# Splitting the next layer's q, k and v columns beside the second MLP product and keeping them in device memory

## The chip, the cores and the metric

The kernel runs on one NeuronCore of a Trainium2 chip. Its instructions stand in five queues, each worked off in order: TensorE (PE in the profile) multiplies matrices, VectorE (DVE) and GpSimd (POOL) do elementwise arithmetic, ScalarE (ACT) does copies and activation functions, SyncE (SP) issues every DMA of this kernel. An instruction starts when it is at the head of its queue and the semaphores that it waits for have come. The metric is the device time of one execution in microseconds (us).

## The reference, cut to what matters

Two encoder layers on 1024 positions of width 1024, in float32. A layer is a token mixing that starts with `u = x @ w_in[l]`, an output product with a LayerNorm, and an MLP with a LayerNorm:

```python
for l in range(DEPTH):                              # DEPTH = 2
    u = x @ w_in[l]
    u_f, q_b, k_b, v_b, u_c, q_d, k_d, v_d = jnp.split(u, pts, axis=-1)
    ...                                             # four kinds of mixing -> y
    x = layer_norm(ALPHA * x + y, ln1_g[l], ln1_b[l])
    h = jnp.square(jax.nn.relu(x @ w_ff1[l]))
    x = layer_norm(ALPHA * x + h @ w_ff2[l], ln2_g[l], ln2_b[l])
```

The case turns on the border between the layers: the end of `h @ w_ff2[0]` with its LayerNorm, and the first products of layer 1, `x @ w_in[1][:, 256:512]` (all of `q_b`) and `x @ w_in[1][:, 512:768]` (`k_b` and `v_b`).

## The kernel before, in words

Every float32 operand of a product is split into a high part that TensorE takes (`F32R`) and a low part, the rest; a product is then three matmuls, hi by hi, hi by lo and lo by hi (`mm3`, lines 172 to 176, shown as L174, L175, L176). A split is `split` (L167): a cast on ACT (L168) gives the high part, a subtraction (L169) on VectorE or GpSimd the low part.

The second MLP product (`ff_down`) uses Strassen's seven products. The 4096 rows of `w_ff2` are taken in 4 chunks, each chunk takes 7 steps in the order `DOWN = (1, 2, 6, 5, 3, 7, 4)`, so there are 28 steps, i = 0 to 27. A step is 4 tiles of 12 matmuls of 512 columns, each tile summed in one of 6 PSUM banks (`x`), and VectorE adds each tile to a running sum (L1540) and so frees its bank. A step needs an operand A (1 MB of hidden values, loaded from `h_scratch` and split in `down_a`, L1414 to L1421: cast on ACT, the first two quarters of the subtraction on GpSimd, the other half on VectorE) and an operand W (split by L168 and L169 on ACT and VectorE from blocks of `w_ff2`). There are three places for each: the operands of step i+3 go where those of step i were, so the load of the next A (`w<-h_scratch` or `T<-h_scratch`) is issued when a step ends, and it serves the step three later.

In the last chunk the sums get their last additions with a running total of each row (`total`, L1440), and then each tile of 128 rows is normalized (`norm`, L1443, and `normalize`, L185: a square on ACT with a sum, L189, a square root, L190, and on VectorE L191, L192 and twice L194, each half stored to `x_scratch`). The tiles 0 to 3 are done after the steps 3 and 7 of the last chunk, the tiles 4 to 7 after its last step. In the order in which the program stands on VectorE, the totals and the norms are mixed with each other.

At the start of the last step the columns of `q_b` for the next layer are loaded into four tiles `raw` (256 KB each; the pool has four such buffers) and split into a tile `w` of a pool with two buffers; the two are also the A operands of the last steps. The columns of `k_b` and `v_b` are loaded into the same four `raw` buffers, and are split at the start of the next layer. These splits use ACT (`CAST w<-raw`) and GpSimd (`TENSOR_TENSOR w<-raw,w`). Then the rows are turned by transposes on TensorE (`back`, L224: L220, and a split from PSUM into `T` on ACT and VectorE), and for each tile of rows comes the product with the columns of `q_b`, three tiles later that with the columns of `k_b` and `v_b` (`mix`, from L336). The order inside each queue is set when the program is built, from the program's order and a schedule; it can differ from the order of the lines.

Of the kernel before, what the change touches and what calls it, by code (L numbers as in the profile page):

```python
# [16 lines left out]
F32R = mybir.dt.float32r  # L17
# [5 lines left out]
P = 128  # L23
# [3 lines left out]
KT = D // P  # L27
DEPTH = 2
# [80 lines left out]
class Trunk:  # L109
    def __init__(self, ctx, tc, a):  # L110
        self.tc, self.nc, self.a = tc, tc.nc, a
        nc = self.nc
        perm = ctx.enter_context(tc.tile_pool(name="perm", bufs=1, side="right"))
        self.ws = ctx.enter_context(tc.tile_pool(name="ws", bufs=1, side="right"))
        self.ps = ctx.enter_context(tc.tile_pool(name="ps", bufs=1, space=PSUM))
        self.ahead = None
        self.T = perm.tile([P, KT, 2, S], F32R, name="T")
        self.ident = perm.tile([P, P], F32, name="ident")
        self.eps = perm.tile([P, 2], F32, name="eps")
        nc.vector.memset(self.eps[:, 0:1], LN_EPS)  # L120
        nc.vector.memset(self.eps[:, 1:2], RMS_EPS)

        def scratch(name, *shape):
            return nc.dram_tensor(name, shape, F32, kind="Internal").ap()

        self.xs = scratch("x_scratch", S, D)
        self.bs = scratch("bias_scratch", 4, P * RL)
        self.ms = scratch("merge_scratch", 2, S, 4)

        self.qd = scratch("q_scratch", 8, 2, HD, S)  # L130
        self.kd = scratch("k_scratch", 6, 2, HD, S)
        self.vd = scratch("v_scratch", S, 6, 2, HD)

        self.tabs = scratch("dft_scratch", 4, P, 2, 2, 2, 2 * P)

        self.hs = scratch("h_scratch", 7, PAIRS, P, 512)


# [106 lines left out]
    def split_cols(self, raws):  # L245
# [2 lines left out]
            self.split(W[:, 2 * i:2 * i + 2, 0], W[:, 2 * i:2 * i + 2, 1], raw, self.nc.gpsimd)  # L248
        return W

    def load_cols(self, w, c0):
        return self.split_cols(self.fetch_cols(w, c0))

# [79 lines left out]
        self.dma(self.vd[t * P:(t + 1) * P, h0:h0 + n], v)  # L333


    def mix(self, l, Wq, raws, before):  # L336
        nc, tc, a = self.nc, self.tc, self.a
        w_in = a["w_in"][l]
        g, v = nc.gpsimd, nc.vector
        with ExitStack() as c:  # L340
# [4 lines left out]
            if Wq is None:  # L345
                Wq = self.load_cols(w_in, 256)
# [4 lines left out]
            for t in range(NT + KLAG):  # L351
                if t < NT:
                    step()
                    o = self.tm([Wq], t)
                    nc.scalar.copy(qk[:, t, 0:4].rearrange("p a b -> p (a b)"), o)
                if t == 0:
                    Wk = self.split_cols(raws or self.fetch_cols(w_in, 512))
                if t == NT:
                    gate = self.load_cols(w_in, 1024)
                if t >= KLAG:  # L360
                    o = self.tm([Wk], t - KLAG)
                    nc.scalar.copy(qk[:, t - KLAG, 4:6].rearrange("p a b -> p (a b)"), o[:, 0:128])
                    self.put_values(sm, o[:, 128:256], t - KLAG, 0, 2)
# [1061 lines left out]
    def ff_down(self, l, places, w2, last, p0, b11):  # L1425
# [8 lines left out]
        junk = kp.tile([P, D], mybir.dt.bfloat16, name="junk")  # L1434
        mvs = [kp.tile([P, 4], F32, name=f"mv{t}") for t in range(NT)]
        out = a["out"] if last else self.xs
        Wq, raws = None, None


        def total(t, j, y):  # L1440
# [7 lines left out]
        with ExitStack() as c:  # L1448
# [58 lines left out]
            for i in range(steps):  # L1507
                ch, n = i // 7, DOWN[i % 7]
                final = ch == steps // 7 - 1
                A, W = places[i % 3]  # L1510
                if final and n == 4 and not last:
                    Wq = self.split_cols(self.fetch_cols(a["w_in"][l + 1], 256))
                    raws = self.fetch_cols(a["w_in"][l + 1], 512)
                if final and n == 7:
                    held = []
                for t in range(4):

                    both = final and n == 4
                    o = held[t] if both else acc.tile([P, 512], F32, tag="x", name="x", bufs=6)
                    for j in range(CHUNK):  # L1520
                        self.mm3(o, [A[:, j, k, t * P:(t + 1) * P] for k in (0, 1)], [W[:, j, k] for k in (0, 1)],
                                 j == 0 and not both, j == CHUNK - 1, both or final and n == 7)
                    r = R[n][t]
                    if ch == 0 and n in (2, 3, 7):
                        v.scalar_tensor_tensor(r, residual(t + 4 * (n == 7), int(n != 2)), ALPHA, o, OP.mult, OP.add)
                    elif ch == 0 and n == 4:

                        y, z = residual(t + 4, 0), residual(t + 4, 1)
                        g.tensor_tensor(y, y, z, OP.subtract)
                        v.scalar_tensor_tensor(r, y, ALPHA, o, OP.mult, OP.add)  # L1530
                    elif ch == 0:
                        act.copy(r, o)
                    elif final and n in (3, 7, 4):
                        total(t + 4 * (n != 3), int(n != 4), o)
                        if n == 3:
                            norm(t)
                        if n == 7:
                            held.append(o)
                    else:
                        v.tensor_tensor(r, o, r, OP.add)  # L1540
                    if not final:
                        continue
                    if n == 1:
                        g.tensor_tensor(R[4][t], R[4][t], R[7][t], OP.add)
                    if n == 2:
                        total(t, 0, R[1][t])
                    if n == 6:
                        v.tensor_tensor(r, r, R[1][t], OP.add)  # L1548
                        g.tensor_tensor(R[4][t], R[4][t], r, OP.add)
                    if n == 5:  # L1550
                        v.tensor_tensor(r, r, R[6][t], OP.add)  # L1551
                        v.tensor_tensor(R[3][t], R[3][t], r, OP.add)  # L1552
                        g.tensor_tensor(R[7][t], R[7][t], r, OP.add)
                if 3 <= i + 3 < steps:
                    prepare2(i + 3)
                if final and n == 1:
                    for k, y in enumerate(("ln2_g", "ln2_b")):
                        self.dma(gb[:, k], a[y][l].rearrange("(o d) -> o d", o=1).to_broadcast([P, D]))
# [14 lines left out]
        if last:  # L1573
            for t in range(4, NT):
                norm(t)
            keep.close()
            return None, None, None
        return Wq, raws, tail()


@with_exitstack
def encoder_kernel(ctx, tc, a):
    tr = Trunk(ctx, tc, a)
    Wq, raws, before = None, None, tr.embed()
    for l in range(DEPTH):
        psum = ExitStack()
        psum.enter_context(tr.wide())
        with tr.third():
            Wo = tr.mix(l, Wq, raws, before)
        Wo = tr.attention(l, Wo)  # L1590
        psum.enter_context(tr.third())
        Wq, raws, before = tr.ff(l, Wo, psum, l == DEPTH - 1)


# [25 lines left out]
```

## Time and profile before

| | us |
|---|---|
| median of 3 runs | 2331.02 (2330.0 to 2331.39) |
| the profiled execution | 2328.44 |
| its span, first to last instruction | 2326.3 |
| PE busy | 2217.1 (95%) |
| DVE busy | 1776.1 (76%) |
| ACT busy | 1077.1 (46%) |
| POOL busy | 793.3 (34%) |

The span is the time from the first to the last instruction of the profiled execution; 2.1 us of the execution lie outside it. TensorE is busy nearly all the time, so the time of the kernel is the time of its matmuls and of the waits in between. The second MLP product of layer 0 ends at about 1171 us of the span, in the middle of it. A row of a timeline gives start, duration, engine, line, operation, what is written and read, how many equal instructions were merged, and in brackets how long the engine had been idle and who released it.

### The profile page before, as it was taken

How to read it: one execution, taken by the hardware profiler on the slowest of the kernel's cores; microseconds unless marked ns; L12 is line 12 of the kernel's file. 1: busy time of each engine (PE TensorE's matmuls, PEld its weight loads, DVE VectorE, ACT ScalarE, POOL GpSimd, SP SyncE). 2: the span in 40 equal slices, each digit the busy share in tenths (PEclk: the TensorE clock that was granted, in tenths of full speed). 3: DMA queues.
4: the chain of work that ended last, by engine and by line, in shares of the span. 5: the costliest groups of instructions: out<-in, count | busy, mean ns of one | idle time of the engine just before them, and what ended most of it. 6: DMA issues, size and time to landing. Idle time of an engine off the chain costs nothing. (4 is left out here: it accounts for less than half of the span.)

```text
span 2326.3 us, 31019 instructions
## 1 busy us (share of the span) xinstructions
PE 2217.1 (95%) x11212; PEld 1869.2 (80%) x11212; DVE 1776.1 (76%) x2500; ACT 1077.1 (46%) x1851; POOL 793.3 (34%) x540
## 2 busy tenths in 40 slices
PE   7999899998999999999989999999899999999997
PEld 6888887976778887888788798788677788788886
DVE  7687667968776777778957966788787767776699
ACT  3343767845333344333333446677443333443333
POOL 2361203016332233435514702110262333354353
PEclk9999999999999999999999999999999999999999
DMA  8444673043344467644223539621343444765433
GB/s 312 127 124 149 190 197 117 19 154 116 137 160 162 159 223 261 205 142 134 98 92 98 153 114 260 171 83 58 125 147 132 165 163 158 276 217 175 160 100 109
DMA packets 222950, 357.44 MB, mean 154 GB/s; under 512 B 21416, under 2 KB 100716, under 8 KB 221708
## 3 DMA queue, kind: packets, MB, share of 16 engines
q1 hardware_dynamic: 222796, 355.45, 47.1%
q8 instruction: 89, 1.46, 0.3%
q14 instruction: 65, 0.53, 0.1%
HBM read 244.44 MB, written 115.15 MB: 155 GB/s over the span
## 5 line engine op out<-in xcount | busy, mean ns | idle before, releaser
L174 PE MATMUL x<-T,w 128*128 128x512 f32 x1088 | 425.5, 393 | 12.2 <-DVE x L1441 4.7
L176 PE MATMUL x<-T,w 128*128 128x512 f32 x1088 | 425.0, 391 | 4.0 <-POOL w L169 2.6
L175 PE MATMUL x<-T,w 128*128 128x512 f32 x1088 | 426.2, 392 | 2.8 <-DVE T L169 2.8
L174 PEld LDWEIGHTS x<-T,w 128*128 128x128 f32 x1088 | 205.3, 189 | 60.8 <-issue 9.7
L176 PEld LDWEIGHTS x<-T,w 128*128 128x128 f32 x1088 | 205.6, 189 | 49.4 <-POOL w L169 3.4
L175 PEld LDWEIGHTS x<-T,w 128*128 128x128 f32 x1088 | 205.7, 189 | 46.7 <-DVE T L169 4.2
L1420 POOL TENSOR_TENSOR w<-w 128x512 fp32r<-128x512 f32 x76 | 147.5, 1961 | 225.1 <-ACT w L1418 225.1
L169 POOL TENSOR_TENSOR w<-raw,w 128x512 fp32r<-128x512 f32 x96 | 138.3, 1466 | 236.7 <-ACT w L168 221.4
L169 POOL TENSOR_TENSOR w<-s,w 128x512 fp32r<-128x512 f32 x68 | 104.3, 1544 | 246.2 <-ACT w L168 165.9
L174 PE MATMUL x<-E,w 128*128 128x512 f32 x384 | 150.6, 392 | 5.9 <-ACT h L1269 4.5
L176 PE MATMUL x<-E,w 128*128 128x512 f32 x384 | 150.1, 392 | 2.0 <-POOL w L169 1.8
L175 PE MATMUL x<-E,w 128*128 128x512 f32 x384 | 150.0, 391 | 0.0
L174 PE MATMUL s<-w,T 128*128 128x256 f32 (+1 forms) x432 | 137.0, 318 | 5.8 <-ACT T L168 5.4
L176 PE MATMUL s<-w,T 128*128 128x256 f32 (+1 forms) x432 | 135.0, 313 | 1.6 <-POOL T L169 1.2
L175 PE MATMUL s<-w,T 128*128 128x256 f32 (+1 forms) x432 | 134.8, 313 | 1.3 <-POOL w L169 1.3
L169 POOL TENSOR_TENSOR w<-rw,w 128x512 fp32r<-128x512 f32 x60 | 93.4, 1573 | 122.5 <-ACT w L168 122.5
L1047 DVE TENSOR_TENSOR s<-rw 128x512 f32<-128x512 f32 x62 | 53.4, 861 | 104.0 <-DMA rw<-in_w_ff_dram 103.7
L1418 ACT CAST w<-w 128x2048 fp32r<-128x2048 f32 x38 | 72.7, 1912 | 129.4 <-DMA w<-h_scratch 122.4
L174 PE MATMUL x<-T 128*128 128x512 f32 x320 | 126.1, 394 | 0.0
L175 PE MATMUL x<-T 128*128 128x512 f32 x320 | 125.5, 392 | 0.0
L176 PE MATMUL x<-T 128*128 128x512 f32 x320 | 125.4, 392 | 0.0
L456 DVE SCALAR_TENSOR_TENSOR o<-hp,cvT,o 128x1024 f32<-128x1024 f32 x88 | 113.3, 1287 | 2.4
(378 smaller groups left out, 5796.5 us busy)
## 6 DMA issues: line engine op xcount, KB each, us to landing
h_scratch<-h SPq DMA_DIRECT2D x224, 256.0 KB, 2.5
w<-h_scratch SPq DMA_DIRECT2D x38, 1024.0 KB, 5.4
rw<-in_w_ff_dram SPq DMA_DIRECT2D x64, 512.0 KB, 5.5
b<-in_w_ff_dram SPq DMA_DIRECT2D x24, 1024.0 KB, 5.5
raw<-x_scratch SPq DMA_DIRECT2D x72, 256.0 KB, 4.7
T<-h_scratch SPq DMA_DIRECT2D x18, 1024.0 KB, 5.3
raw<-in_w_in_dram SPq DMA_DIRECT2D x64, 256.0 KB, 3.5
rw<-in_w_ff_dram SPq DMA_DIRECT2D x10, 1024.0 KB, 5.3
```

The lines of the kernel that those rows point to most:

```text
L169: (lo_eng or self.nc.vector).tensor_tensor(lo, src, hi.bitcast(F32), OP.subtract)
L174: mm(out, l[0], r[0], start=first, stop=False, skip_group_check=more)
L175: mm(out, l[0], r[1], start=False, stop=False, skip_group_check=more)
L176: mm(out, l[1], r[0], start=False, stop=last, skip_group_check=more)
L456: v.scalar_tensor_tensor(o, hp[:, m, k:k + S], cvT[:, m, k:k + 1], o, OP.mult, OP.add)
L1047: eng.tensor_tensor(quad(out), x, y, op)
L1418: nc.scalar.copy(A[:, :, 0], f32)
L1420: nc.gpsimd.tensor_tensor(A[:, j, 1], f32[:, j], A[:, j, 0].bitcast(F32), OP.subtract)
```

## The change

A scratch array in device memory (`w_scratch`) is added. In the steps 8 to 15 of the second MLP product of layer 0, `put_cols` takes a quarter of the q columns (steps 8 to 11) or of the k and v columns (steps 12 to 15): a load of 256 KB into a `raw` buffer, a cast on ACT and a subtraction on GpSimd into two more `raw` buffers, and two stores of 256 KB to `w_scratch`. At the start of the last step `get_cols` loads the split q columns with two DMAs of 1 MB into a tile `w`, and the next layer loads the k and v columns in the same way. The 8 loads, 8 casts and 8 subtractions that stood at the border of the layers are gone. The call of `norm(t)` for the tiles 0 to 3 moves from step 3 to step 7 of the last chunk.

```diff
+        self.wd = scratch("w_scratch", 2, P, KT, 2, 256)
...
+    def put_cols(self, l, j, k):
+        raw, hi, lo = self.raw(), self.raw().bitcast(F32R), self.raw().bitcast(F32R)
+        self.dma(raw, self.a["w_in"][l].rearrange("(k p) n -> p k n", p=P)[:, k:k + 2, 256 + 256 * j:512 + 256 * j])
+        self.split(hi, lo, raw, self.nc.gpsimd)
+        for i, x in enumerate((hi, lo)):
+            self.dma(self.wd[j, :, k:k + 2, i], x)
+
+    def get_cols(self, j):
+        W = self.ws.tile([P, KT, 2, 256], F32R, tag="w", name="w", bufs=2)
+        for k in range(0, KT, 4):
+            self.dma(W[:, k:k + 4], self.wd[j, :, k:k + 4])
+        return W
...
-                    Wk = self.split_cols(raws or self.fetch_cols(w_in, 512))
+                    Wk = self.get_cols(1) if l else self.load_cols(w_in, 512)
...
                 if final and n == 4 and not last:
-                    Wq = self.split_cols(self.fetch_cols(a["w_in"][l + 1], 256))
-                    raws = self.fetch_cols(a["w_in"][l + 1], 512)
+                    Wq = self.get_cols(0)
...
                         total(t + 4 * (n != 3), int(n != 4), o)
-                        if n == 3:
+                        if n == 7:
                             norm(t)
-                        if n == 7:
                             held.append(o)
...
                 if 3 <= i + 3 < steps:
                     prepare2(i + 3)
+                if not last and 8 <= i < 16:
+                    self.put_cols(l + 1, i // 4 - 2, 2 * (i % 4))
```

Where the built program puts these instructions is seen in the queues. The first place is the DMA queue on SP from the steps 8 to 10 on, before the change: `w_7659`, `T_64` and `w_7660` are the places of the operand A, `rw` and `b` blocks of `w_ff2`, `raw` the small buffers.

```order
L141 DMA w_7659<-h_scratch 128x4x512
L141 DMA raw_9726<-in_w_in_dram 128x2x256
L141 DMA raw_9728<-in_w_in_dram 128x2x256
L141 DMA raw_9730<-in_w_in_dram 128x2x256
L141 DMA raw_9732<-in_w_in_dram 128x2x256
L141 DMA T_64<-h_scratch 128x4x512
L141 DMA rw_8501<-in_w_ff2_dram 128x4x512
L141 DMA w_7660<-h_scratch 128x4x512
L141 DMA b_8630<-in_w_ff2_dram 128x4x512
```

The same place after the change, from the first of the eight puts on (`raw_8505` is its load, `raw_8506` its high part, `raw_8507` its low part):

```order
L143 DMA w_scratch<-raw_8506 128x2x256
L143 DMA raw_8577<-in_w_in_dram 128x2x256
L143 DMA w_scratch<-raw_8507 128x2x256
L143 DMA T_64<-h_scratch 128x4x512
L143 DMA w_scratch<-raw_8578 128x2x256
L143 DMA raw_8652<-in_w_in_dram 128x2x256
L143 DMA w_scratch<-raw_8579 128x2x256
L143 DMA rw_8501<-in_w_ff2_dram 128x4x512
L143 DMA w_scratch<-raw_8653 128x2x256
L143 DMA raw_8725<-in_w_in_dram 128x2x256
L143 DMA w_scratch<-raw_8654 128x2x256
L143 DMA w_7660<-h_scratch 128x4x512
```

Each load of an operand A now stands behind two stores of high or low parts and a load; the pattern goes on so through four loads of A (`T_64`, `w_7660`, `w_7659`, `T_64`), with two puts to each. On GpSimd the eight subtractions of the puts stand two by two behind the two subtractions of an operand A, on ACT each cast of a put stands before or behind the cast of an A.

The second place is ACT at the border of the layers, before the change (`x4` to `x7` are the tiles 4 to 7 of the rows, `mv` their sums, `w_9911` the k and v columns, `T_64<-tr` the split of the turned rows of tile 0, in two halves):

```order
L189 ACTIVATE junk_7826,mv4_7831<-x4_7821,mv4_7831 128x1024
L190 ACTIVATE mv4_7831<-mv4_7831,eps_66 128x1
L189 ACTIVATE junk_7826,mv5_7832<-x5_7822,mv5_7832 128x1024
L190 ACTIVATE mv5_7832<-mv5_7832,eps_66 128x1
L168 CAST w_9911<-raw_9743 128x2x256
L189 ACTIVATE junk_7826,mv6_7833<-x6_7823,mv6_7833 128x1024
L168 CAST w_9911<-raw_9745 128x2x256
L168 CAST w_9911<-raw_9747 128x2x256
L168 CAST w_9911<-raw_9749 128x2x256
L168 CAST T_64<-tr_9815 128x4x128
L168 CAST T_64<-tr_9822 128x4x128
```

And after it:

```order
L191 ACTIVATE junk_7826,mv4_7831<-x4_7821,mv4_7831 128x1024
L192 ACTIVATE mv4_7831<-mv4_7831,eps_66 128x1
L191 ACTIVATE junk_7826,mv5_7832<-x5_7822,mv5_7832 128x1024
L192 ACTIVATE mv5_7832<-mv5_7832,eps_66 128x1
L191 ACTIVATE junk_7826,mv6_7833<-x6_7823,mv6_7833 128x1024
L170 CAST T_64<-tr_9857 128x4x128
L170 CAST T_64<-tr_9864 128x4x128
```

The four casts of the k and v columns are gone from among the squares, and the split of tile 0 follows the square of tile 6 at once. (The lines of the changed kernel are 2 to 16 higher.) On VectorE nothing moves with `norm(t)`: totals and norms stand in the same order as before, and only two splits `T_64<-tr` stand one place earlier.

## Rows read from the trace of the kernel before

**Rows 1.** Waits of PE, 1000 to 1260 us: engine, line, waited for: total, times, longest.
```profile
PE x L174 <- DVE x L1441: 2.3, 1, 2.3
PE s L174 <- ACT T L168: 5.2, 1, 5.2
PE tr L220 <- DVE T L169: 1.0, 1, 1.0
```

**Rows 2.** Timeline of PE at the border of the layers.
```profile
1158.51 0.47 PE L174 MATMUL x<-T,w 128*128 128x512 f32 x1 [2.31 <-DVE x L1441]
...
1177.31 0.58 PE L174 MATMUL s<-w,T 128*128 128x256 f32 x1 [5.16 <-ACT T L168]
...
1179.09 1.11 PE L220 MATMUL tr<-ident,x 128*128 128x128 f32 x4 [0.99 <-DVE T L169]
```

**Rows 3.** Stretches: length, busy PE, PEld, DVE, ACT, POOL, then granted PE clock.
```profile
1158.40:1163.00 4.60, 4.49 (x13) 3.57 (x14) 4.60 (x9) 3.00 (x7) 3.05 (x2) 0.63 0.31 114
1177.20:1183.00 5.80, 4.70 (x21) 4.41 (x22) 5.76 (x8) 2.75 (x7) 3.48 (x3) 0.50 0.76 219
1283.40:1290.00 6.60, 6.57 (x29) 5.44 (x30) 6.49 (x6) 4.08 (x6) 6.60 (x6) 1.00 0.28 86
```

**Rows 4.** Timeline of ACT at the border.
```profile
1173.99 1.15 ACT L189 ACTIVATE junk<-x,mv 128x1024 bf16<-128x1024 f32 x1 [1.23 <-DVE mv L1445]
...
1175.13 1.64 ACT L168 CAST w<-raw 128x512 fp32r<-128x512 f32 x3
1176.68 1.06 ACT L168 CAST T<-tr 128x512 fp32r<-128x512 f32 x2
```

**Rows 5.** Timeline of DVE at the border.
```profile
1158.28 1.40 DVE L194 SCALAR_TENSOR_TENSOR x<-x,mv,gb 128x512 f32<-128x512 f32 x2
...
1160.22 2.10 DVE L192 SCALAR_TENSOR_TENSOR x<-x,mv,gb 128x1024 f32<-128x1024 f32 x1
...
1162.91 2.82 DVE L194 SCALAR_TENSOR_TENSOR x<-x,mv,gb 128x512 f32<-128x512 f32 x2
...
1168.50 1.28 DVE L192 SCALAR_TENSOR_TENSOR x<-x,mv,gb 128x1024 f32<-128x1024 f32 x1 [1.31 <-ACT junk L189]
...
1178.36 1.27 DVE L169 TENSOR_TENSOR T<-tr,T 128x512 fp32r<-128x512 f32 x2
```

**Rows 6.** Timeline of POOL at the border.
```profile
1159.95 6.94 POOL L169 TENSOR_TENSOR w<-raw,w 128x512 fp32r<-128x512 f32 x4 [11.28 <-ACT w L168]
```

**Rows 7.** Timeline of SP's DMA issues, steps 7 to 13.
```profile
949.55 0.37 SPq L141 DMA_DIRECT2D T<-h_scratch  x1
...
960.38 0.37 SPq L141 DMA_DIRECT2D w<-h_scratch  x1
...
1014.83 0.36 SPq L141 DMA_DIRECT2D T<-h_scratch  x1
```

**Rows 8.** Timeline of POOL, steps 8 and 9.
```profile
949.86 3.84 POOL L1420 TENSOR_TENSOR w<-w 128x512 fp32r<-128x512 f32 x2 [4.11 <-ACT w L1418]
...
967.88 3.58 POOL L1420 TENSOR_TENSOR w<-w 128x512 fp32r<-128x512 f32 x2 [7.36 <-ACT w L1418]
```

**Rows 9.** Line 169: duration ns min/median/max, first and last start us, form.
```profile
L169 POOL TENSOR_TENSOR w<-raw,w x96: 1269/1298/2802, 11.6 to 1538.0; 128x512 fp32r<-128x512 f32 x96
...
L169 DVE TENSOR_TENSOR T<-b,T x30: 2272/2292/3378, 890.0 to 2286.5; 128x2048 fp32r<-128x2048 f32 x30
```

**Rows 10.** Timeline of DVE, steps 11 and 12.
```profile
989.67 1.23 DVE L1421 TENSOR_TENSOR T<-T 128x1024 fp32r<-128x1024 f32 x1 [1.39 <-ACT T L1418]
...
1007.14 1.27 DVE L1540 TENSOR_TENSOR x<-x,x 128x512 f32<-128x512 f32 x2
```

**Rows 11.** A stretch over steps 12 to 14, columns as in Rows 3.
```profile
995.00:1028.00 33.00, 33.00 (x148) 27.31 (x147) 31.38 (x26) 11.57 (x7) 10.58 (x6) 1.00 0.30 101
```

**Rows 12.** DMA issues: count, KB each, median us from issue to landing.
```profile
raw<-x_scratch SPq DMA_DIRECT2D x72, 256.0 KB, 4.7
...
h_scratch<-h SPq DMA_DIRECT2D x224, 256.0 KB, 2.5
```

More of the change, by code (lines that the diff above doesn't have):

```diff
@@ L333, in put_values, with mix @@
         self.dma(self.vd[t * P:(t + 1) * P, h0:h0 + n], v)
-    def mix(self, l, Wq, raws, before):
+    def mix(self, l, Wq, before):
         nc, tc, a = self.nc, self.tc, self.a
@@ L1436, in ff_down @@
         out = a["out"] if last else self.xs
-        Wq, raws = None, None
+        Wq = None
         def total(t, j, y):
@@ L1576, in ff_down @@
             keep.close()
-            return None, None, None
-        return Wq, raws, tail()
+            return None, None
+        return Wq, tail()
 @with_exitstack
@@ L1583, in encoder_kernel @@
     tr = Trunk(ctx, tc, a)
-    Wq, raws, before = None, None, tr.embed()
+    Wq, before = None, tr.embed()
     for l in range(DEPTH):
@@ L1588, in encoder_kernel @@
         with tr.third():
-            Wo = tr.mix(l, Wq, raws, before)
+            Wo = tr.mix(l, Wq, before)
         Wo = tr.attention(l, Wo)
         psum.enter_context(tr.third())
-        Wq, raws, before = tr.ff(l, Wo, psum, l == DEPTH - 1)
+        Wq, before = tr.ff(l, Wo, psum, l == DEPTH - 1)
 _INS = ['x', 'emb_ln_g', 'emb_ln_b', 'w_in', 'w_fnet', 'q_norm_g', 'k_norm_g', 'conv_dw', 'conv_b',
```

## Prediction

> **What bounds the kernel now.** The time is that of TensorE's matmuls and of what they wait for, so I read the waits of PE first, around the place that the change touches. From 1000 to 1260 us the view lists three waits and no other [rows 1]: 2.3 us before the last step of the second MLP product, for a total on VectorE; 5.2 us before the first product of layer 1, for the split of the turned rows on ACT; and 1.0 us for the low part of the same split. Together 8.46 us; all three lie at the border of the layers, none in the steps before it.
>
> Then the timelines of the border, one engine after the other. PE is released at 1158.51, 1177.31 and 1179.09 [rows 2]. ACT shows why the second is so late: the square of tile 6 starts at 1173.99 and takes until about 1175.1, then three casts of the k and v columns (1.64 us) stand ahead of the split of tile 0, which starts at 1176.68 [rows 4]. VectorE is late as well: while GpSimd subtracts the q columns (four in 6.94 us from 1159.95, [rows 6]), L192 takes 2.10 us instead of 1.28 and two L194 take 2.82 instead of 1.40 [rows 5]. After the waits the granted clock is lower: 0.50, the level of 1.2 GHz, from 1177.2 to 1183.0, and 0.63 on average after the wait of 2.31 us [rows 3].
>
> Last the queues in the steps 8 to 14, where the puts go. A load of an operand A is issued when a step ends: at 949.55, 960.38 and 1014.83, the first and the last six steps apart, so a step takes 10.88 us [rows 7]. From the issue at 960.38 to the first subtraction on GpSimd at 967.88 are 7.50 us (landing and cast), and the two subtractions take 3.58 us [rows 7, 8]: A is ready 11.1 us after its issue. The load issued at the end of step i serves step i+3, which starts two steps or 21.8 us later. So each A is ready 10.7 us ahead. That is the cover behind which the puts would be free.
>
> **The change, part one: the border (a gain).** The casts and subtractions of the q, k and v columns go. On VectorE the L192 loses 0.82 us and the L194 pair 1.42 us of hindrance [rows 5], so that the total that follows comes about 2.2 us sooner. From there the totals, the squares on ACT and the norms follow each other as before, each about 2.3 us sooner (the last step's matmuls, which end where they did, allow it: their first tile is done at about 1163, the third at 1168.5). The square of tile 6 then runs from about 1171.7 to 1172.9 and the split of tile 0 follows it at once: 1172.9 instead of 1176.68, and PE starts at about 1173.5 instead of 1177.31, 3.8 us sooner. The low part on VectorE (1178.36, [rows 5]) comes behind L192 of tile 6, which has also lost a hindrance of 0.4 us and starts 2.5 to 3 us sooner: about 1174.8, 3.6 us sooner, and with it the third wait. I take 3.7 us. What is late next there is the wait for VectorE's total at 1158.51, which stays: nothing of it lies behind the removed work. The lowered clock from 1177.2 to 1183.0 costs half of 5.8 us, 2.9 us [rows 3]; with shorter waits it may stay away or come again, so half of it, 1.4 us. Sum: 5.1 us gained, between 2 and 6.6.
>
> Costed at nothing: the q columns' two loads of 1 MB. In SP's order they stand behind the two halves of tile 3, at about 1163.2 and 1163.8; a load of 1 MB is landed and cast 7.5 us after its issue [rows 7, 8], so the first is there well before 1170.7, the second a few us later, and the first product takes its half up only after half of its matmuls. Without that cover the first product would wait for the rest. The k and v columns wait for the last step (about 1171) and land by 1180, the product with them starts over 10 us later. The move of `norm(t)`: nothing, as VectorE's order is the same.
>
> **Part two: the eight puts (a loss).** In TensorE's time they are nothing; the question is what they do to the loads of A, since in SP's queue each load of A now stands behind the store of a low part, which waits for a subtraction on GpSimd, which stands behind the two subtractions of the A before. That closes a ring, from one load of A to the next: 7.50 us to the first subtraction, 3.58 us for the two [rows 7, 8], the put's subtraction, and 0.4 us for the issue of the store. The put's subtraction takes 1.30 us by itself [rows 9]. But ACT casts W right behind A and the put, so VectorE's subtraction for W (2.29 us, [rows 9]) comes in at the same moment, and the trace shows VectorE and GpSimd taking turns: 1.29 us become 2.3 beside a subtraction of 1.23 us (3.58 for two, [rows 8]). So 1.3 to 3.6 us; I take 3.5, since the casts on ACT put the two side by side. One turn of the ring: 7.5 + 3.6 + 3.5 + 0.4 = 15.0 us, at the least 12.8. A step is 10.88.
>
> About the two engines the Trainium skill says more (SBUF — State Buffer, Who interferes with whom): a VectorE instruction with two SBUF inputs and a GpSimd instruction that reads SBUF exclude each other, and the second blocks until the first has finished. The stretched pairs of rows 8 agree. By that rule the put's subtraction waits for all of the 2.29 us and a turn is 15.0 us; if both only ran at half speed, it would take 2.6 us and a turn 14.1.
>
> The start: the first put's subtraction stands behind the two that start at 949.86 and take 3.84 us [rows 8], so it ends at about 955.0, and the load of A for step 10 goes out at 955.5 instead of 949.55. It is ready at 966.6, step 10 starts at 971.3: no wait. The next three go out at 970.5, 985.5 and 1000.5 and are ready at 981.6, 996.6 and 1011.6; the steps 11, 12 and 13 want them at 982.2, 993.1 and 1004.0. So TensorE waits 3.5 us before step 12 and 4.2 more before step 13: 7.7 us by then. With turns of 12.8 us it is 1.1.
>
> Then VectorE. It had subtracted A of step 13 at 989.67 [rows 10], and now does so 7.5 us after 1000.5, at 1008.0. Behind it in its queue stand the additions of step 12, whose last two (1007.14, [rows 10]) free the banks that step 14 needs at 1014.83. The 17.5 us between the two rows hold only about 2.8 us of idleness (VectorE is busy for 31.4 of 33 us there, [rows 11]), so the additions come at about 1022.7 and end after 1023.4; step 14, put back by 7.7, would start at 1022.5. That is 0.9 us more, and more again if GpSimd's late subtractions hinder VectorE here: 2 us, between 0 and 5.
>
> The waits are then three or four, of 2 to 4 us. After 2.31 us the clock fell, after 2.70 us (before 1283.43) it did not [rows 3]. At the lower level the 4.6 us after the first cost about 1.7 us; for half of three or four waits I take 2.4 us, between 0 and 5.
>
> The stores to `w_scratch` do not occur before. The nearest rows are 2.5 us for a store of 256 KB and 4.7 us for a load of that size in company [rows 12]; they hold the `raw` buffers of later puts. At 2.5 they are hidden in the turn, at 4.7 they would add about 2 us to a turn. I take 2.5.
>
> Sum: 7.7 + 2 + 2.4 - 5.1 = 7.0 us slower. The profiled execution would be 2335.4 instead of 2328.44. That one is 2.6 us below the median of the runs, which I take as the base: 2338.0.
>
> **The rivals.**
>
> *The ring never closes (faster).* If a turn is at most 12.4 us, the 4.7 us by which step 10's operand is ahead last for the three turns and TensorE never waits in the steps. That needs the put's subtraction to come through in 1 us, or loads and casts 0.4 us quicker than 7.5. For it: the engines are idle for half of these steps, and GpSimd busy for 3.58 of 10.88. Against it: the queues are in order. The border's gain remains: 2331.0 - 5.1 = 2326.
>
> *A short ring (no change).* Turns of 12.8 to 13.5 us, when VectorE's subtraction for W does not come in between: 1.1 to 3.2 us of waits, VectorE then late by 0 to 2, one lowered clock at most: -4 to +1, about 2329.
>
> *A longer ring.* Stores and loads in one queue at 4.7 us: turns of 17 us, three of them 6 us more, and longer waits at the low clock: 2338 + 8 = 2346.
>
> *The border waits for the q columns.* If the stores of the norms hold the two loads up by 5 us, the gain there is lost: 2338 + 5 = 2343. Against it: by the reckoning above the first is there some 3 us early.
>
> That the norms of the first tiles come later is a step that changes no order; it has no price in any case.
>
> **How the numbers follow.** 0.2% is 4.7 us, about what a measurement of this kernel tells from no change. The forecast has 0.47, and its own range is 2333 to 2343; the ring that never closes 0.15, the short ring 0.20, the longer ring 0.12, the late columns 0.06. Slower by over 0.2% (above 2335.7) are the last two and most of the forecast, 0.58; within it the short ring and the low end of the forecast, 0.27; faster the first, 0.15. The range is 2327 to 2346: it leaves out most of the first rival and the far end of the third.
>
> **What would show it.** In the profile after: PE waits at the starts of the steps 12, 13 and 14 of layer 0's second MLP product, some 3 to 5 us each, where there were none, released by VectorE or GpSimd; loads of A on SP about 15 us apart from 955 to 1001, instead of 10.9; the split of tile 0 on ACT right behind the square of tile 6, and PE's wait there under 3 us. Wrong would be the forecast if the loads of A stay 11 to 12 us apart, or if PE waits at the border for a DMA.

## The result and the profile after

The changed kernel takes 2341.53 us (median of 7 runs, 2338.23 to 2349.91) against 2329.87 us of the kernel before, run beside it (7 runs, 2321.55 to 2331.39): a ratio of 1.0058, 95% interval 1.004 to 1.0076. It is slower by 11.7 us in the medians and by 13.5 us (9.3 to 17.7) by the ratio. The forecast was 2338.0 us, 7.0 slower, in a range from 2327 to 2346.

The profiled execution of it is its longest run (2349.91 us, span 2348.0), so I compare stretches and not spans. TensorE executes the same 11,212 matmuls in both, and two stretches between their starts carry the change: from matmul 4440 to 5300 (the steps 3 to 21 of the second MLP product of layer 0, with all puts) 210.2 us instead of 194.9, 15.3 more; from 5544 to 5800 (step 26, the border and the first product of layer 1) 46.6 instead of 50.5, 3.9 less. 15.3 - 3.9 = 11.4 us is near the difference of the medians. The rest of the longer span, 4.5 us before matmul 4440 and 5.8 us behind matmul 5800, I leave out: over the fourteen kernels of this document, which run nearly the same instructions there, the first part takes 895.6 to 905.5 us and the second 1121.9 to 1130.6, in no order that follows their edits.

The waits of PE in the steps, from 940 to 1060 us, where the kernel before had none that the view lists:

```profile
PE x L176 <- DVE x L1554: 5.1, 2, 3.3
PE x L176 <- DVE r L1554: 4.4, 2, 3.9
```

(Columns: the waiting line, what released it, us in total, times, longest.) With two more of 0.3 us that is 10.1 us, all but 0.6 of it released by VectorE's additions, which free the banks. SP's queue shows where they come from. These are the loads of A, each with the store of a low part that stands ahead of it (start, us of the issue, queue, line, operation):

```profile
960.47 0.36 SPq L143 DMA_DIRECT2D w_scratch<-raw  x1
960.88 0.46 SPq L143 DMA_DIRECT2D T<-h_scratch  x1
...
976.25 0.36 SPq L143 DMA_DIRECT2D w_scratch<-raw  x1
976.70 0.42 SPq L143 DMA_DIRECT2D w<-h_scratch  x1
...
992.10 0.36 SPq L143 DMA_DIRECT2D w_scratch<-raw  x1
992.55 0.42 SPq L143 DMA_DIRECT2D w<-h_scratch  x1
```

The next load follows at 1008.21. So the loads are 15.82, 15.85 and 15.66 us apart, against 10.88 in [rows 7], and each goes out 0.4 us after a store that was waiting. What it waited for stands in GpSimd's timeline (L1436 the two subtractions of an A, L171 that of a put):

```profile
969.24 5.73 POOL L1436 TENSOR_TENSOR T<-T 128x512 fp32r<-128x512 f32 x2 [6.77 <-ACT T L1434]
974.94 1.28 POOL L171 TENSOR_TENSOR raw<-raw 128x512 fp32r<-128x512 f32 x1
...
985.21 3.56 POOL L1436 TENSOR_TENSOR w<-w 128x512 fp32r<-128x512 f32 x2 [6.98 <-ACT w L1434]
988.73 3.35 POOL L171 TENSOR_TENSOR raw<-raw 128x512 fp32r<-128x512 f32 x1
```

One turn can be read off: load at 976.70, first subtraction at 985.21 (8.5 us later), two of them 3.5, the put's 3.35 to 992.08, the next load at 992.55. Then VectorE, which had subtracted its half of A early in [rows 10], now idles for it and has the additions behind it:

```profile
1000.83 1.23 DVE L1437 TENSOR_TENSOR w<-w 128x1024 fp32r<-128x1024 f32 x1 [8.71 <-ACT w L1434]
1001.97 1.28 DVE L1554 TENSOR_TENSOR r<-x,r 128x512 f32<-128x512 f32 x2
```

PE starts step 12 at 1002.80, behind the first of these additions. The granted clock behind the two longer waits and at the border (columns as in [rows 3]):

```profile
1003.80:1007.20 3.40, 3.39 (x8) 2.15 (x7) 3.40 (x3) 0.00 (x0) 3.40 (x2) 0.50 0.08 27
1020.80:1024.20 3.40, 3.40 (x8) 2.73 (x9) 3.40 (x3) 0.00 (x0) 0.00 (x0) 0.51 1.04 386
1178.45:1183.00 4.55, 4.55 (x20) 3.77 (x21) 4.55 (x10) 0.80 (x3) 0.00 (x0) 1.00 0.31 115
1194.90:1198.30 3.40, 2.87 (x14) 2.87 (x15) 3.36 (x7) 1.91 (x4) 0.00 (x0) 0.50 0.95 361
```

In the steps it fell to half, 1.2 GHz, behind waits of 3.91 us (ending at 1002.80) and 3.30 us (ending at 1019.10). At the border it stayed at 2.4 GHz behind a wait of 2.48 us and fell behind one of 2.97. The two stretches of 3.4 us at half speed in the steps cost 3.4 us together; with the waits that is 13.5 of the 15.3 us. The other 1.8 lie in short gaps beside the waits. At the border PE's waits, which answer to [rows 2], and ACT, which answers to [rows 4]:

```profile
1178.42 0.47 PE L176 MATMUL x<-T,w 128*128 128x512 f32 x1 [2.48 <-DVE x L1457]
1193.43 0.38 PE L176 MATMUL s<-w,T 128*128 128x256 f32 x1 [2.97 <-ACT T L170]
1195.43 1.12 PE L222 MATMUL tr<-ident,x 128*128 128x128 f32 x4 [1.50 <-DVE T L171]
```

```profile
1191.66 1.15 ACT L191 ACTIVATE junk<-x,mv 128x1024 bf16<-128x1024 f32 x1 [1.74 <-DVE mv L1461]
...
1192.81 1.05 ACT L170 CAST T<-tr 128x512 fp32r<-128x512 f32 x2
```

The split of tile 0 follows the square of tile 6 at once. From the wait before the last step to the first product it is 15.01 us (1193.43 - 1178.42) instead of 18.80 [rows 2]. VectorE is no longer hindered: its L194 takes 1.27 us and its pair of L196 1.40, where [rows 5] had 2.10 and 2.82. The first row here is VectorE's last split of a block of `w_ff2`, the last row its first split of turned rows:

```profile
1162.20 2.28 DVE L171 TENSOR_TENSOR T<-b,T 128x2048 fp32r<-128x2048 f32 x1
...
1180.14 1.27 DVE L194 SCALAR_TENSOR_TENSOR x<-x,mv,gb 128x1024 f32<-128x1024 f32 x1
...
1182.00 1.40 DVE L196 SCALAR_TENSOR_TENSOR x<-x,mv,gb 128x512 f32<-128x512 f32 x2
...
1194.69 0.69 DVE L171 TENSOR_TENSOR T<-tr,T 128x512 fp32r<-128x512 f32 x1
```

From the first to the last of these rows it is 32.49 us, in which VectorE idles once, for 1.31 us. I call this stretch VectorE's chain. Before the change it took 36.08 us, with the same one gap of 1.31 us, from this row to 1178.36 in [rows 5]:

```profile
1142.28 2.28 DVE L169 TENSOR_TENSOR T<-b,T 128x2048 fp32r<-128x2048 f32 x1
```

### The profile page after: what moved, and what is told of

The parts are those of the page before. It is cut to its first block, busy times and chain, and to the rows that moved or that the text cites. A ratio compares the mean times of both kernels' runs of the same rounds, so it can differ in the third digit from the quotient of the medians.

```text
span 2348.0 us, 31066 instructions
## 1 busy us (share of the span) xinstructions
PE 2223.9 (95%) x11212; PEld 1872.1 (80%) x11212; DVE 1780.8 (76%) x2500; ACT 1075.8 (46%) x1851; POOL 798.2 (34%) x540
## 5 line engine op out<-in xcount | busy, mean ns | idle before, releaser
L1436 POOL TENSOR_TENSOR w<-w 128x512 fp32r<-128x512 f32 x76 | 149.5, 1987 | 211.5 <-ACT w L1434 209.5
L171 POOL TENSOR_TENSOR w<-raw,w 128x512 fp32r<-128x512 f32 x88 | 124.7, 1442 | 223.0 <-ACT w L170 219.3
L171 POOL TENSOR_TENSOR w<-s,w 128x512 fp32r<-128x512 f32 x68 | 103.5, 1533 | 250.4 <-ACT w L170 171.4
L171 POOL TENSOR_TENSOR w<-rw,w 128x512 fp32r<-128x512 f32 x60 | 93.5, 1575 | 122.7 <-ACT w L170 122.7
```

Source lines behind the costliest of these rows:

```text
L171: (lo_eng or self.nc.vector).tensor_tensor(lo, src, hi.bitcast(F32), OP.subtract)
L1436: nc.gpsimd.tensor_tensor(A[:, j, 1], f32[:, j], A[:, j, 0].bitcast(F32), OP.subtract)
```

## The experiments

Twelve kernels ran, each beside the kernel before on the same chip. The last three columns are read from their profiles: the two stretches of TensorE and VectorE's chain.

| kernel | median us (before) | ratio, 95% interval | 4440 to 5300 | 5544 to 5800 | chain |
|---|---|---|---|---|---|
| before | 2329.87 | 1 | 194.9 | 50.5 | 36.08 |
| the change | 2341.53 (2329.87) | 1.0058, 1.004 to 1.0076 | 210.2 | 46.6 | 32.49 |
| e1 border alone | 2325.28 (2326.03) | 0.9997, 0.998 to 1.0014 | 194.9 | 47.4 | 32.48 |
| e2 puts alone | 2343.81 (2326.03) | 1.0073, 1.0054 to 1.0092 | 212.1 | 51.1 | 36.10 |
| e3 stores later | 2326.39 (2326.03) | 0.9995, 0.9982 to 1.0008 | 194.9 | 48.4 | 32.47 |
| e4 stores ahead | 2352.22 (2326.03) | 1.0114, 1.0093 to 1.0135 | 222.6 | 49.4 | 32.49 |
| e5 GpSimd's queue | 2332.06 (2325.09) | 1.0025, 1.0009 to 1.0041 | 205.3 | 47.8 | 32.49 |
| e6 two ahead | 2324.50 (2325.09) | 0.9992, 0.9977 to 1.0008 | 194.9 | 47.5 | 32.49 |
| e7 four ahead | 2340.56 (2325.09) | 1.006, 1.0041 to 1.008 | 212.3 | 48.8 | 32.50 |
| e8 subtract twice | 2361.20 (2325.09) | 1.0144, 1.0123 to 1.0164 | 230.3 | 46.8 | 32.49 |
| e9 e3, norms behind | 2322.15 (2327.27) | 0.9974, 0.9957 to 0.9991 | 194.9 | 43.8 | 30.07 |
| e10 before, norms behind | 2322.69 (2327.27) | 0.9977, 0.9965 to 0.999 | 194.9 | 44.6 | 30.61 |
| e11 e9, norms two ahead | 2321.12 (2328.34) | 0.9968, 0.9953 to 0.9984 | 194.9 | 42.8 | 26.96 |
| e12 norm call alone | 2325.79 (2328.34) | 0.9991, 0.9975 to 1.0006 | 194.9 | 49.9 | 36.07 |

**The two halves apart: e1 and e2.** e1 fills `w_scratch` without puts, with plain copies, and leaves the split out:

```diff
-                if not last and 8 <= i < 16:
-                    self.put_cols(l + 1, i // 4 - 2, 2 * (i % 4))
+                if not last and 16 <= i < 20:
+                    self.fill_cols(i - 16)   # one 1 MB copy w_in -> w_scratch
```

> Without the eight puts; w_scratch is filled by four copies of 1 MB within device memory, one behind each load of A of four later steps (the columns are then not split, which this kernel leaves out of the computation); the border is that of the changed kernel. My theory (the loss lies in the steps, the border gains): 3.6 to 5 us faster than before, 2325 to 2326.5 us, PE's waits in the steps 8 to 15 none, at the border some 5 us in place of 8.5. Rival A (the border itself brings nothing or loses, since the q columns come late): within 1 us of before or slower, with a wait of PE for a DMA at the border.

The steps lose nothing, and the border is 3.1 us shorter in the profile (50.5 - 47.4), but of that the runs show 0.7 us, with an interval from 4.7 us faster to 3.3 slower. That is a miss by size: 3.6 to 5 was expected. By its time alone Rival A (within 1 us of before) would stand. Its mechanism does not: no wait of PE there is for a DMA.

e2 puts the eight puts into the kernel before.

```diff
                     prepare2(i + 3)
+                if not last and 8 <= i < 16:
+                    self.put_cols(l + 1, i // 4 - 2, 2 * (i % 4))
```

> The border as before, and the eight puts in the steps as in the changed kernel, their results not used. My theory: the puts alone cost what the two aligned traces give, 15 us by the steps 11 to 14 (of it 10 in waits of PE, the rest low clock): 2342 to 2346 us, loads of A 15 to 16 us apart. If the loss came from the border or from the reads of w_scratch: near before, 2330.

It is 17.0 us slower by the ratio and 17.2 us longer in the steps, as expected. The whole loss is in the puts. Its border is that of the kernel before, and it shows something on the wait that [rows 1] gave as 5.2 us:

```profile
PE s L176 <- ACT T L170: 6.8, 1, 6.8
...
PE x L176 <- DVE x L1450: 2.2, 1, 2.2
```

Here the clock stayed at 2.4 GHz behind the wait of 2.2 us (granted 1.00 from 1172.2 to 1180.0), the last step was over sooner, and the next wait was longer by as much: the stretch is 51.1 us against 50.5.

**The order on SP: e3 and e4.** Both have one put to a load of A and the same order on ACT, GpSimd and VectorE up to the border. In e3 the two stores of a put are issued behind the next load of A, in e4 ahead of it. In both the load of a put is queued behind the load of A of its step. The edits, cut to the lines that place the stores:

```diff
# e3
+            self.store_cols()                     # issues the stores of the put before
         self.split(hi, lo, raw, self.nc.gpsimd)
-        for i, x in enumerate((hi, lo)):
-            self.dma(self.wd[j, :, k:k + 2, i], x)
+        self.late = [(self.wd[j, :, k:k + 2, i], x) for i, x in enumerate((hi, lo))]
# e4
+                self.stored = self.dma(self.wd[j, :, k:k + 2, i], x)
...
+        with self.tc.issue_after(self.stored.ins) if self.stored else nullcontext():
+            self.gate_ = self.dma(A[:, :, 1], ...)    # the next load of A
```

> All the work of the changed kernel, one put to a load of A; the two stores of a put stand in the DMA queue behind the next load of A but ahead of nothing that waits for them. My theory (the loads of A were held in the queue by the stores): loads of A 10.9 us apart again, no wait of PE in the steps, 2325 to 2327 us, as e1. Rival B (the puts' transfers and the hindrance between VectorE and GpSimd cost the time, wherever they stand): 5 to 12 us over that, 2331 to 2338. Rival C (the ACT and GpSimd work of the puts delays the operands A by 3 us each, enough with their place in those queues): some waits of 1 to 2 us stay, 2328 to 2331.

> As e3, with the same order on ACT and GpSimd, but the two stores of a put stand ahead of the next load of A. My theory: the ring closes once per step, eight turns of 13 to 15 us against steps of 10.9; less the 10.7 us by which the operands are ahead that is 6 to 22 us of waits, so 2333 to 2348 us, and most likely 2340. Rivals B and C: the puts are as far apart as in e3 and do the same work, so the time is that of e3 within 2 us.

e3's loads of A:

```profile
969.89 0.37 SPq L144 DMA_DIRECT2D w<-h_scratch  x1
980.73 0.36 SPq L144 DMA_DIRECT2D T<-h_scratch  x1
```

Beside the puts they are 10.83 to 10.89 us apart, PE has no wait in the steps, and the stretch takes 194.9 us, as before to the tenth. e4:

```profile
991.95 8.97 SPq L145 DMA_DIRECT2D w_scratch<-raw  x2
1001.34 0.36 SPq L145 DMA_DIRECT2D w<-h_scratch  x1
```

Its eight turns, from a load at 955.42 to one at 1079.34, take 123.9 us, 36.9 more than eight steps; less the cover of 10.7 that is 26.2, and the stretch is 27.7 us longer. The same work, one put to a load of A, costs the steps nothing or 27.7 us (26.5 by the ratio), by the place of the stores in one queue. Rivals B and C (transfers, hindrance, places on ACT and GpSimd) are out for this loss. At 2352.22 us e4 lies beyond the 2333 to 2348 that I gave: its turns are 15.5 us on average and not 13 to 15.

e3 is not free of late loads, though. Behind its last puts:

```profile
1043.58 4.85 SPq L144 DMA_DIRECT2D raw<-in_w_in_dram  x2
1048.52 0.42 SPq L144 DMA_DIRECT2D T<-h_scratch  x1
...
1059.14 1.02 SPq L144 DMA_DIRECT2D raw<-in_w_in_dram  x2
1060.26 0.41 SPq L144 DMA_DIRECT2D w<-h_scratch  x1
```

These two loads of A come 13.4 and 11.7 us after the ones before them, 3.4 us late together. Ahead of them stand loads into `raw` that belong to no put and wait until the buffers are free: for the landing of stores (1043.56, 1059.12, 1059.78) and for the end of a put's subtraction (1048.03). TensorE does not notice, since the cover is 10.7 us. VectorE does: it idles 6.9 and 5.6 us for its halves of these operands, and from there its queue has no gap of more than 0.3 us up to the start of its chain at the border.

**The cover: e6 and e7.** The first two, or four, puts as in e4, the others as in e3.

```diff
+            self.stored = self.store_cols() if m < 2 else None    # e7: m < 4
```

> As e3 and e4, the stores of the first two puts ahead of the next load of A, the other six later. My theory (lateness adds up over consecutive turns and is free as long as the cover of 10.7 us lasts): the first turns of e4 were 12.9 and 15.5 us, so the loads are 6.6 us late at the most and TensorE waits nowhere in the steps: time of e3, 2324 to 2328 us. Rival E (each such turn costs its excess): 6.6 us more, 2332 to 2334.

```profile
957.94 0.36 SPq L145 DMA_DIRECT2D w<-h_scratch  x1
...
970.65 0.42 SPq L145 DMA_DIRECT2D w<-h_scratch  x1
...
986.07 0.42 SPq L145 DMA_DIRECT2D T<-h_scratch  x1
...
990.54 0.37 SPq L145 DMA_DIRECT2D w<-h_scratch  x1
```

Turns of 12.71 and 15.42 us, 6.4 us late, made up with the next load 4.5 us later; PE waits nowhere. Rival E is out.

> As e6, the stores of the first four puts ahead. My theory: turns of 12.9, 15.5, 17.6 and 15.9 us as in e4 make the fourth load 18.4 us late, 7.7 us beyond the cover: one or two waits of PE, 6 to 9 us together, and some low clock: 2332 to 2337 us. Rival E: 18 us, 2344.

e7 came out above my range, between the two. Its four runs do not separate them (14.0 us over before by the ratio, 9.5 to 18.6); the profile does. The first turn was 17.05 us and not 12.9: 17.05 + 15.51 + 17.72 + 15.89 less four steps is 22.7 us late, 12.0 beyond the cover. PE's waits in the steps:

```profile
PE x L178 <- DVE x L1567: 9.0, 1, 9.0
PE x L180 <- POOL T L1449: 3.8, 2, 2.2
```

Of these 1.65 us (ending at 1001.50) and the 9.0 lie in the four turns, 10.7 us; 2.2 us (ending at 1080.62) come later. Behind two of them the granted clock was half for 3.4 us each. 9.0 + 3.8 + 3.4 = 16.2 of the 17.4 us by which the stretch is longer. The account by the cover asks for 12.0 us of waits in the four turns and 10.7 were found; the turn that I had put into it was too short.

**The link itself: e8 and e5.** e8 is e4 with the subtraction of the put carried out twice.

```diff
             self.split(hi, lo, raw, self.nc.gpsimd)
+            self.nc.gpsimd.tensor_tensor(lo, raw, hi.bitcast(F32), OP.subtract)
```

> As e4, the subtraction of each put carried out twice. My theory: each of the eight turns becomes longer by the second subtraction, 1.3 us alone and up to 3.5 beside VectorE, and the cover is used up already: turns of 17 to 19 us, 10 to 28 us over e4, 2363 to 2380, likeliest 2366. If the turns were set by the transfers (landing of A beside stores) and not by GpSimd: within 3 us of e4, 2352.

Seven turns from 957.89 to 1076.75 take 16.98 us each, against 15.49 of the first seven in e4: 1.5 more, near the 1.3 of one unhindered subtraction [rows 9]. The stretch grows by 7.7 us over e4, the ratio by 0.3%, 7.0 us, with an interval of some 5 us to either side of each of the two ratios. So it is the turns in the profiles that speak against the rival of the transfers, and not the times alone. It is the direction of my theory, below its size (in e8 the eighth load of A went ahead of the last store, so only seven turns count). In e5 the stores go through GpSimd's own queue:

```diff
-            self.dma(self.wd[j, :, k:k + 2, i], x)
+            self.nc.gpsimd.dma_start(self.wd[j, :, k:k + 2, i].bitcast(F32), x.bitcast(F32))
```

> The changed kernel, two puts to a load of A, with the stores of the high and low parts issued on GpSimd's own DMA queue instead of SP's. My theory (SP held the loads of A behind stores that waited for GpSimd): loads of A 10.9 us apart, no PE waits in the steps, 2325 to 2328 us. Rival D (the ring lies in the engines' own queues, or issuing stores costs GpSimd so much that its subtractions for A come late): turns over 12 us remain, waits of several us, 2332 to 2345.

My theory missed: e5 is 5.8 us slower by the ratio, at the near end of Rival D, and turns of mostly over 12 us remain. The profile gives another reason than Rival D's. On SP the load of a `raw` buffer now stands ahead of the load of A and waits (first GpSimd, then SP, then SP's waits for the landing of stores):

```profile
960.45 3.21 POOL L171 TENSOR_TENSOR raw<-raw 128x512 fp32r<-128x512 f32 x1 [0.48 <-DMA w_scratch<-raw]
```

```profile
963.68 0.37 SPq L143 DMA_DIRECT2D raw<-in_w_in_dram  x1
...
964.67 0.45 SPq L143 DMA_DIRECT2D w<-h_scratch  x1
...
1014.08 5.37 SPq L143 DMA_DIRECT2D raw<-in_w_in_dram  x4
1019.51 0.46 SPq L143 DMA_DIRECT2D w<-h_scratch  x1
```

```profile
SPq L143 <- DMA w_scratch<-raw: 13.3, 3, 5.0
```

The loads at 963.68 and 1014.08 go out when a put's subtraction ends (963.66, 1014.06); the last of the four at 1014.08 waits until a store has landed (1018.96). So my theory was too narrow: not the stores alone hold up A, but whatever stands ahead of it in SP's queue and waits, for GpSimd's data or for a buffer that GpSimd or a store still holds. The late loads in e3 are of the second kind as well. The turns are shorter (13.96, 12.75, 11.68, 13.11, then 17.30), late by 14.4 us in the end. Less the cover that is 3.7 us, and the steps are 10.4 us longer. In three of these turns the 1 MB of A is also slower, 10.7, 7.6 and 12.2 us from issue to cast against 5.3 to 5.6 in the steps 8 to 12 before; why, and how much of the loss that is, no run separates. More `raw` buffers would test the wait for a buffer alone; that was not run.

**The border: e9, e10, e11.** The chain is 32.5 us in all eight kernels with the changed border up to here, whatever PE's waits were. I took it that VectorE's queue sets the end there, and moved behind it what need not stand there. The edit moves the squares of the norms on ACT as well, so it does not separate the two queues; for VectorE speaks that it idles 1.31 us in its chain, while ACT waits for it before the square of tile 6 (1.74 us).

```diff
-                    self.back(t, rows[t])
-                    norm(t + 4)
+                    hi, lo = self.back(t, rows[t])
+                    with self.tc.issue_after(hi.ins), self.tc.issue_after(lo.ins):
+                        norm(t + 4)
```

> e3 (stores later), and at the border the norms of the tiles 4 to 7 are queued on ACT and VectorE behind the splits of the turned rows of the tiles 0 to 3, one after each. My theory of the border: it is bound by VectorE's queue (32.5 us without a gap but one from the last split of a block of w_ff2 to the first split of turned rows, in e1 and e3 alike, 36.1 before the change), of which the norms of the tiles 4, 5 and 6, about 9 us, need not stand there; PE's two waits there, 2.9 us in e3 and 4.3 in e1, shrink to under 1.5: 1.5 to 3 us less than e3, 2322 to 2325 us. Rival F (the norms are only moved, and the product waits for them before tile 4): the time of e3 or up to 3 us more, 2326 to 2329.

> The kernel before, with only the order of the norms of the tiles 4 to 7 changed as in e9. My theory: the casts of the k and v columns still stand ahead of the split on ACT and GpSimd still hinders VectorE, but the norms of three tiles no longer do: PE's wait of 5.2 us before the first product shrinks by 2 to 4 us: 2322 to 2325 us, so that this reorder by itself brings as much as the whole change of the border. Rival F: no gain, 2325 to 2329.

Waits of PE at the border, e9 and then e10:

```profile
PE x L177 <- DVE x L1465: 3.4, 1, 3.4
...
PE s L177 <- ACT T L171: 0.2, 1, 0.2
```

```profile
PE s L174 <- ACT T L168: 2.4, 1, 2.4
PE x L174 <- DVE x L1442: 2.0, 1, 2.0
```

Both are faster than the kernel before, by 6.1 and 5.4 us (ratios; their intervals end 2.1 and 2.3 us below before), and e9 is faster than the changed kernel, with intervals that lie well apart. Rival F is out. e10 has no part of the change: between it and e9 the times show no difference, so the reorder alone gives all of the gain that can be told. e11 moves the norms of the tiles 2 and 3 too:

```diff
-                        if n == 7:
+                        if n == 7 and (last or t < 2):
                             norm(t)
...
+                        norm(t + 2)     # behind the split of tile t, in place of norm(t + 4)
```

> e9, and the norms of the tiles 2 and 3 as well go behind the splits of the turned rows: norm t+2 behind the split of tile t. In e9 VectorE's queue is still without a gap up to the split of tile 0 (30.1 us from the last split of a block), and the total that PE waits for before the last step (3.4 us) stands behind a norm of tile 2. My theory: both norms, 6 us of VectorE, leave that stretch; PE's wait of 3.4 us shrinks to under 2 and the split of tile 0 is bound by TensorE's last step: 1 to 3 us less than e9, 2319 to 2322 us. Rival F: the norms now lag behind the product tile by tile (4.7 us of VectorE for each against 3.75 of TensorE), so that PE waits before the tiles 2 to 7 and the time is that of e9 or up to 4 us more, 2322 to 2327.

```profile
PE x L177 <- DVE x L1465: 2.1, 1, 2.1
PE tr L223 <- DVE T L172: 1.3, 2, 1.1
```

It is the fastest, 0.9968 (0.9953 to 0.9984), 7.5 us faster than before. That it beats e9 is 1.0 us in the profile (43.8 to 42.8) and not shown by the intervals, which overlap; a later wait of 1.1 us has come up, for a split that stands behind a norm on VectorE, a little of Rival F.

e12 is the one part of the change that no other run has alone:

```diff
-                        if n == 3:
+                        if n == 7:
                             norm(t)
```

> The kernel before with the call of norm(t) in step 7 of the last chunk instead of step 3, and nothing else of the change. The queues of all engines hold the same instructions in the same order as before, so every theory expects the time of before, within 3 us: this run shows how far two runs of equal queues lie apart.

e12 came out at 0.9991, 2.1 us faster, and its interval holds no change. A ratio off 1 by 0.1% here is what two kernels of equal queues show; those of e1, e3 and e6 (0.9997, 0.9995, 0.9992) are no further off, so that the runs show no gain of the changed border.

## Why the prediction was right, step by step

**Right: the ring, its place and its waits.** The loads of A are 15.7 to 15.9 us apart (15.0 forecast), PE waits 3.9, 3.3 and 1.8 us at the starts of the steps 12 to 14, released by VectorE, 10.1 us with the short waits (9.7 forecast). The order on SP is shown as the cause by e3 and e4, the cover by e6. In the changed kernel itself the load of step 13's operand goes out 21.5 us later than before (counted from matmul 4440); less the cover of 10.7 that is 10.8, and step 13 starts 10.9 us later.

**Right: the turn's subtractions.** Two of A and one of the put take 6.9 to 7.0 us of GpSimd (5.73 + 1.28; 3.56 + 3.35), forecast 7.1. The trace agrees with the rule of the Trainium skill that I weighed (SBUF — State Buffer, Who interferes with whom): the put's 3.35 us are nearer to its 3.5 than to the 2.6 of half speed.

**Too small: the turn's 7.5 us from the load to the first subtraction, and the start.** I took the 7.5 us from a load with no company [rows 7, 8]. In the three turns it is 8.4, 8.5 and 8.3 us, with a put's load and stores around it; in e3 and e4, with one put to a load, 7.7 to 8.7, mostly near 8.1. That the transfers in company do it fits this order, but no run has them alone. The steps 12 and 13 start 5.4 and 10.9 us later than before, where I had 3.5 and 7.7. Of the 3.2 us that were missing at step 13, the turns (15.8 us for 15.0) make 2.3, and 0.9 is the first load of the four, which went out 6.8 us late and not 6.0. From step 13 to step 14 it is 4.3 us more, near my 2 for VectorE's additions (the wait there is 1.8) and 2.4 for the clock (3.4 in all, half of it already before step 13). Together 15.3 for 12.1.

**Right in its mechanism, too large in its sum: the border.** The chain became 3.6 us shorter in eight kernels, and the first product comes 3.6 us sooner, where 3.7 was forecast. Of the 1.4 us for the clock behind it only 0.3 came. The lower level lasts 3.4 us there (1194.90 to 1198.30) instead of 5.8 [rows 3], but the third wait has grown from 0.99 to 1.50 us: it seems that part of the slow matmuls had lain beside VectorE's queue and had cost nothing. The same is seen at the first wait. In e2 and e12, with the border of before, the clock stayed high behind it, and the stretch is the same within 0.6 us (51.1 and 49.9 against 50.5). PE's waits became little shorter, 7.0 us instead of 8.46, because all three go back to one queue.

What of the 3.6 us reaches the end differs from kernel to kernel, 1.1 to 3.9 us in the profiles. Most of it is where VectorE's chain starts: in the changed kernel, e1, e5 and e8 8.6 to 8.8 us before matmul 5544, as before the change (8.76), and there the stretch is 2.7 to 3.9 us shorter; in e6, e3, e7 and e4 7.9, 7.1, 6.7 and 5.9 us before it, and it is 3.0, 2.1, 1.7 and 1.1 us shorter. In these four VectorE's queue has had no gap of more than 0.3 us since it idled for late operands some 80 us before, as told for e3, and comes to the border late; in the other four it idled last some 31 us before. That is read from the profiles and not tested by a run. In the times a gain of the border by itself is not shown: e1, e3 and e6 have 0.7, 1.2 and 1.9 us by their ratios, each with an interval of some 3 to 4 us around it, and e12, without any part of it in its queues, has 2.1.

Sum: forecast 12.1 - 5.1 = 7.0; measured 15.3 - 3.9 = 11.4 in the profiles and 11.7 in the medians. Two terms were too favourable: the landing of A in the turn with the start of the ring, 3.2 us, and the clock at the border, 1.1. That the time of 2341.53 is only 3.5 us above my 2338.0 is in part luck, since the kernel before ran 1.2 us below the base that I had added to.

**The rivals.** The ring closed, and it was not short. The longer ring was nearer than I gave it credit for: the turns of 15.8 us lie between its 17 and my 15.0, and its reason, transfers in company, fits the 8.4 us above. The late q columns did not occur: PE waits for no DMA at the border.

**The move of norm(t)** is a step without effect, as forecast: e12 has the same queues as before, and only when e9 and e11 forced the order did the norms come later.

## What to carry to other kernels

SP issued its DMAs in the order of its queue, so a transfer with slack became late as soon as one stood ahead of it that waited for an engine's result or for a buffer (e4 against e3, e5). Put such stores behind the next load that matters, and count what they wait for over several turns against the cover. A load that is late within the cover of one engine can still put another behind, as VectorE in e3. And where several short waits of TensorE go back to one engine that hardly idles, their sum is not the price: measure that engine's chain, and take out of its queue what is needed later.

## What was not expected of the hardware

A store issued on GpSimd's queue takes 0.73 us of GpSimd for one (e5, two of them 1.45), against mostly 0.36 to 0.5 us on SP's queue (e3).

```profile
963.96 0.73 POOL L259 DMA_DIRECT2D w_scratch<-raw  x1 [0.30 <-POOL raw L171]
```

And a fall of the clock to half, behind the wait of 2.31 us [rows 3], cost no measurable time at the border. In e12 the clock stayed high behind a wait of 2.2 us, and the next wait, which goes back through ACT to VectorE, was 6.8 us instead of 5.2.
